# Row maxima on one core: the last two rows in three pieces, and GpSimd on 128-wide parts of ten late rows

## The chip, the cores and the metric

One core of a Trainium2 chip. The time is device microseconds of one execution (us), lower is better. Most executions of a kernel agree within a few tenths of a per cent. So each time is a median of several executions.

## The reference

```python
batch, seq, dim = 32, 512, 1024
x = np.random.randn(batch, seq, dim).astype(np.float32)
return np.max(x, axis=-1).astype(np.float32)
```

That is 16,384 rows of 1024 values, 67.1 MB read and 64 KB written. The kernel lays 128 rows in each of the 128 partitions. In this text "a row" is one row in every partition, 1024 values by 128 partitions, 512 KB.

## The kernel before

SyncE issues 22 loads into a ring of 46 rows, a buffer that is filled over and over. The loads get smaller towards the end. VectorE reduces each load with one instruction. Near the end GpSimd takes five whole rows off VectorE: TensorE transposes the row, ScalarE copies it out of PSUM, the memory that TensorE writes, GpSimd takes the maximum across the partitions, and TensorE brings the result back ("back"), where VectorE reduces eight values per row ("merge").

```python
BLOCKS = [
    [15, 15, 15, 13, 13, 11, 9, 9, 6, 6],
    [3, 3, 2, 1, 1, 1, 1, 1, 1, 1],
]
RING = 46
BY_GPSIMD = {8: 1, 9: 3, 12: 1}        # load: its last rows that GpSimd takes, whole
MERGE = {9: 8, 15: 9, 18: 12}          # after load 9 merge load 8's rows, ...
...
    ring = once.tile([P, RING, D], F32)
    res = once.tile([P, I], F32)
...
            nc.sync.dma_start(out=xc, in_=xb[:, b:b + n, :])
            ...
            reduce = in_turn("DVE", nc.vector.reduce_max(
                out=cols[:, :n - m], in_=xc[:, :n - m, :], axis=X))
...
    half = ring[:, at, :H]
    nc.sync.dma_start(out=half, in_=xb[:, b, :H])
    nc.sync.dma_start(out=tail[:, PAD:], in_=xb[:, b, H:])
    in_turn("DVE", nc.vector.reduce_max(out=tail[:, PAD - 1:PAD], in_=half, axis=X))
    in_turn("DVE", nc.vector.reduce_max(out=res[:, I - 1:], in_=tail[:, PAD - 1:], axis=X))
```

The last row comes in two halves. The maximum of the first half is written just in front of the second, so that one reduction of 513 values finishes the row.

## Time and profile before

| | before |
|---|---|
| time, median (lowest to highest) | 164.42 us (164.33 to 164.50, 3 runs); with later runs of the same kind 164.37 us (6 runs) |
| span of the profiled run | 162.6 us |
| VectorE busy | 135.0 us, 83% |
| load queue busy | 96.6% of the span |
| VectorE idle, waiting for loads | 24.3 us |
| GpSimd busy | 16.3 us |

Two resources are nearly full, the transfers and, from 57 us on, VectorE. The load queue's share says that no other order of the same loads can end much earlier. VectorE's share is an average over a start where it waits and an end where it doesn't. The lines themselves stand in the prediction below.

### The profile page before, as it was taken

To read this page: it belongs to the slowest core of one execution; us is meant where nothing else is said; L and a number is where in the kernel's file an instruction comes from. 1 tells how busy PE (TensorE), PEld (TensorE's weight loads), DVE (VectorE), ACT (ScalarE), POOL (GpSimd) and SP (SyncE) were. 2 spreads that over 40 slices of the span, in tenths; PEclk is the share of its full clock that TensorE was granted. 3 is DMA by queue.
4 is the path that set the end of the run, shared out by engine and by line. 5 is a ranking of instruction groups with operands and counts; after the bars stand their busy time and mean duration, and the time that the engine had idled before them with its cause. 6 is when DMAs were issued, how large, how long until landed. Compare 5 with 4: busy or idle time off the path is not lost.

```text
span 162.6 us, 293 instructions
## 1 busy us (share of the span) xinstructions
PE 13.0 (8%) x80; PEld 11.7 (7%) x80; DVE 135.0 (83%) x33; ACT 6.3 (4%) x6; POOL 16.3 (10%) x9
## 2 busy tenths in 40 slices
PE   0000000000000000000000000000000040943520
PEld 0000000000000000000000000000000030933420
DVE  3000079995999779999996999999999999999994
ACT  3000000000000000000000000000000011240200
POOL 0000000000000000000000000000000007099910
PEclk9999999999999999999999999999999999985555
DMA  7999699988999799999998989999999999999990
GB/s 242 484 484 438 287 484 484 484 378 348 484 484 484 333 498 432 445 419 419 419 419 387 499 388 427 417 426 408 417 435 435 471 399 426 423 418 409 406 368 16
DMA packets 3456, 67.18 MB, mean 413 GB/s; under 512 B 640, under 2 KB 640, under 8 KB 1792
## 3 DMA queue, kind: packets, MB, share of 16 engines
q1 hardware_dynamic: 3168, 67.11, 96.6%
q10 hardware_dynamic: 288, 0.07, 0.2%
HBM read 67.11 MB, written 0.07 MB: 413 GB/s over the span
## 4 chain that ended last, share of the span: by engine, by line
DVE 54%; DMA 44%; SPq 0%; issue 0%
DVE res L139 53%; DMA ring<-in_x_dram 44%; DVE res L156 0%; DVE tail L155 0%; SPq L133 0%; DVE res L143 0%
## 5 line engine op out<-in xcount | busy, mean ns | idle before, releaser
L139 DVE TENSOR_REDUCE res<-ring 128x1 f32<-128x1024 f32 (+6 forms) x20 | 132.1, 6653 | 24.3 <-DMA ring<-in_x_dram 24.3
L106 POOL PARTITION_ALL_REDUCE top<-sb x5 | 16.1, 3255 | 138.8 <-ACT sb L104 138.8
L98 PE MATMUL ps<-ident,ring 128*128 128x128 f32 x40 | 8.1, 382 | 134.2 <-DMA ring<-in_x_dram 131.8
L98 PEld LDWEIGHTS ps<-ident,ring 128*128 128x128 f32 x40 | 7.1, 204 | 134.3 <-issue 134.2
L104 ACT COPY sb<-ps 128x1024 f32<-128x1024 f32 x5 | 5.1, 1013 | 144.9 <-PE ps L98 143.0
L115 PE MATMUL fetched<-ident,top 1*128 1x1 f32 x40 | 5.0, 243 | 9.1 <-POOL top L106 9.1
L115 PEld LDWEIGHTS fetched<-ident,top 1*128 1x128 f32 x40 | 4.6, 214 | 10.3 <-POOL top L106 9.8
L104 ACT ACT_TABLE_LOAD x1 | 1.3, 1283 | 0.7 <-PEq L176 0.7
L76 DVE MEMSET ident<- 128x128 f32 x1 | 0.2, 165 | 0.8 <-PEq L176 0.8
L156 DVE TENSOR_REDUCE res<-tail 128x1 f32<-128x513 f32 x1 | 0.7, 686 | 0.0
L155 DVE TENSOR_REDUCE tail<-ring 128x1 f32<-128x512 f32 x1 | 0.7, 675 | 0.0
L83 DVE TENSOR_SCALAR rowno<-rowno 32x1 f32<-32x1 f32 x3 | 0.4, 147 | 0.1
L143 DVE TENSOR_REDUCE res<-fetched 128x1 f32<-128x8 f32 (+1 forms) x3 | 0.5, 161 | 0.0
L78 DVE TENSOR_TENSOR_SCAN colno<-ident 128x128 f32<-128x128 f32 x1 | 0.4, 425 | 0.0
L85 DVE TENSOR_SCALAR ident<-colno,rowno 128x128 f32<-128x128 f32 x1 | 0.3, 287 | 0.0
L80 DVE STREAM_TRANSPOSE rowno<-colno 128x32 f32<-128x32 f32 x1 | 0.2, 211 | 0.0
L176 POOL MEMSET const-float32-0.0<- 128x1 f32 x1 | 0.1, 99 | 0.2 <-issue 0.2
L176 POOL MEMSET const-uint8-127<- 128x1 uint8 x1 | 0.1, 103 | 0.0
L176 POOL MEMSET const-bfloat16-1.0<- 128x1 bf16 x1 | 0.1, 102 | 0.0
L176 POOL MEMSET const-float32-1.0<- 128x1 f32 x1 | 0.1, 99 | 0.0
L77 DVE MEMSET rowno<- 128x32 f32 x1 | 0.1, 85 | 0.0
## 6 DMA issues: line engine op xcount, KB each, us to landing
ring<-in_x_dram SPq DMA_DIRECT2D x3, 7680.0 KB, 38.4
ring<-in_x_dram SPq DMA_DIRECT2D x2, 6656.0 KB, 34.6
ring<-in_x_dram SPq DMA_DIRECT2D x2, 4608.0 KB, 37.8
ring<-in_x_dram SPq DMA_DIRECT2D x2, 3072.0 KB, 31.9
ring<-in_x_dram SPq DMA_DIRECT2D x1, 5632.0 KB, 28.6
ring<-in_x_dram SPq DMA_DIRECT2D x7, 512.0 KB, 22.3
ring<-in_x_dram SPq DMA_DIRECT2D x2, 1536.0 KB, 34.9
ring<-in_x_dram SPq DMA_DIRECT2D x1, 1024.0 KB, 33.4
```

Of the source, the lines that this page charges most:

```text
L78: in_turn("DVE", nc.vector.tensor_tensor_scan(out=colno, data0=ident, data1=ident, initial=-1.0, op0=ALU.add, op1=ALU.mult))
L83: in_turn("DVE", nc.vector.tensor_scalar(out=part, in0=part, scalar1=float(q * 32), scalar2=None, op0=ALU.add))
L85: in_turn("DVE", nc.vector.tensor_scalar(out=ident, in0=colno, scalar1=rowno[:, 0:1], scalar2=None, op0=ALU.is_equal))
L98: in_turn("PE", nc.tensor.transpose(out=ps[:, c * P:(c + 1) * P], in_=rows[:, k, c * P:(c + 1) * P], identity=ident,))
L104: nc.scalar.copy(out=sb, in_=ps)
L106: nc.gpsimd.partition_all_reduce(top, sb, P, bass_isa.ReduceOp.max)
L115: in_turn("PE", nc.tensor.transpose(out=backs[j][:, k, c:c + 1], in_=tops[j, k][0:1, c * P:(c + 1) * P], identity=ident[0:1, 0:1],))
L139: reduce = in_turn("DVE", nc.vector.reduce_max(out=cols[:, :n - m], in_=xc[:, :n - m, :], axis=X))
L143: in_turn("DVE", nc.vector.reduce_max(out=tiles[i][1], in_=backs[i], axis=X))
L155: in_turn("DVE", nc.vector.reduce_max(out=tail[:, PAD - 1:PAD], in_=half, axis=X))
L156: in_turn("DVE", nc.vector.reduce_max(out=res[:, I - 1:], in_=tail[:, PAD - 1:], axis=X))
L176: nc = _bacc.Bacc("TRN2", target_bir_lowering=False, num_devices=1)
```

## The change

It has four parts. VectorE gets its rows in 21 loads instead of 22, of other sizes. GpSimd takes the first three 128-wide parts (384 of 1024 values) of ten late rows, 3.75 rows' worth, in place of five whole rows, and VectorE the other 640 values. The last two rows come in three pieces of 689, 671 and 688 values, and the middle piece holds the end of one row and the start of the next, so that one reduction with two results serves both. The first store waits for the reduction of the middle piece. The sizes of two buffer pools and the program order of some instructions change with this.

```diff
 BLOCKS = [
-    [15, 15, 15, 13, 13, 11, 9, 9, 6, 6],
-    [3, 3, 2, 1, 1, 1, 1, 1, 1, 1],
+    [15, 15, 15, 13, 11, 9, 8, 5, 8, 7, 6],
+    [4, 3, 2, 2, 1, 1, 1],
 ]
-BY_GPSIMD = {8: 1, 9: 3, 12: 1}
-MERGE = {9: 8, 15: 9, 18: 12}
+SHARED = {10: (5, 3), 12: (3, 3), 14: (2, 3)}    # load: (rows, 128-wide parts)
+MERGE = {13: (10,), 16: (12,), 19: (14,)}
...
+    W = 336
+    K = W - 1
+    AT = I + 16
+    MID = AT + K + W + 17
+    res = once.tile([P, MID + D - W], F32)
...
+        if n > m:
+            maximum(res[:, col:col + n - m], rows(j)[:, :n - m, :])
+        if m and parts < C:
+            maximum(share(j)[:, parts, :], rows(j)[:, n - m:, parts * P:])
+        merge(j)
...
-    half = ring[:, at, :H]
-    nc.sync.dma_start(out=half, in_=xb[:, b, :H])
-    nc.sync.dma_start(out=tail[:, PAD:], in_=xb[:, b, H:])
-    in_turn("DVE", nc.vector.reduce_max(out=tail[:, PAD - 1:PAD], in_=half, axis=X))
-    in_turn("DVE", nc.vector.reduce_max(out=res[:, I - 1:], in_=tail[:, PAD - 1:], axis=X))
+    piece = ring[:, at, :D - K]
+    nc.sync.dma_start(out=piece, in_=xb[:, S - 2, :D - K])
+    pair = xb[:, S - 2:, :].rearrange("p i d -> p (i d)")
+    nc.sync.dma_start(out=res[:, AT:AT + K + W], in_=pair[:, D - K:D + W])
+    nc.sync.dma_start(out=res[:, MID:], in_=pair[:, D + W:])
+    maximum(res[:, AT - 1:AT], piece)
+    latest_row = maximum(
+        bass.AP(tensor=res.tensor, offset=res.offset + I - 2,
+                ap=[list(res.ap[0]), [MID - 1 - (I - 2), 2]]),
+        res[:, AT - 1:AT + K + W].rearrange("p (r k) -> p r k", r=2))
+    merge(len(loads) + 1)
+    maximum(res[:, I - 1:I], res[:, MID - 1:])
```

More of the change, by code (lines that the diff above doesn't have):

```diff
@@ L13 @@
 BLOCKS = [
-    [15, 15, 15, 13, 13, 11, 9, 9, 6, 6],
-    [3, 3, 2, 1, 1, 1, 1, 1, 1, 1],
+    [15, 15, 15, 13, 11, 9, 8, 5, 8, 7, 6],
+    [4, 3, 2, 2, 1, 1, 1],
 ]
 RING = 46
-TENSOR = {
-    8: [("turn", 8, 0), ("back", 8, 0)],
-    9: [("turn", 9, 0), ("turn", 9, 1), ("turn", 9, 2), ("back", 9, 0)],
-    12: [("turn", 12, 0), ("back", 9, 1), ("back", 9, 2), ("back", 12, 0)],
-}
-BY_GPSIMD = {8: 1, 9: 3, 12: 1}
-MERGE = {9: 8, 15: 9, 18: 12}
+SHARED = {10: (5, 3), 12: (3, 3), 14: (2, 3)}
+TENSOR = [
+    ("turn", 10, 0), ("turn", 10, 1), ("turn", 10, 2), ("back", 10, 0),
+    ("back", 10, 1), ("turn", 12, 0), ("turn", 12, 1), ("back", 10, 2),
+    ("turn", 14, 0), ("back", 12, 0), ("back", 12, 1), ("back", 14, 0),
+]
+MERGE = {13: (10,), 16: (12,), 19: (14,)}
 NOSYNC = mybir.DependencyInfo(mybir.DependencyClass.NoSync, mybir.DependencyReason.DATA)
@@ L53 @@
     allr = ctx.enter_context(tc.tile_pool(name="allr", bufs=2))
-    psum = ctx.enter_context(tc.tile_pool(name="psum", bufs=3, space=bass.MemoryType.PSUM))
-    psmall = ctx.enter_context(tc.tile_pool(name="psmall", bufs=2, space=bass.MemoryType.PSUM))
+    psum = ctx.enter_context(tc.tile_pool(name="psum", bufs=2, space=bass.MemoryType.PSUM))
+    psmall = ctx.enter_context(tc.tile_pool(name="psmall", bufs=4, space=bass.MemoryType.PSUM))
     ring = once.tile([P, RING, D], F32)
-    res = once.tile([P, I], F32)
-    PAD = 16
-    tail = once.tile([P, PAD + H], F32)
+    W = 336
[3 more added lines that the diff above has]
+    res = once.tile([P, MID + D - W], F32)
     latest = {}
@@ L86 @@
         out=ident, in0=colno, scalar1=rowno[:, 0:1], scalar2=None, op0=ALU.is_equal))
-    tiles = {}
-    tops = {}
-    backs = {}
-    def turn(j, k):
-        rows, cols = tiles[j]
-        ps = psum.tile([P, D], F32)
-        for c in range(C):
-            in_turn("PE", nc.tensor.transpose(
-                out=ps[:, c * P:(c + 1) * P],
-                in_=rows[:, k, c * P:(c + 1) * P],
-                identity=ident,
-            ))
-        sb = turned.tile([P, D], F32)
-        nc.scalar.copy(out=sb, in_=ps)
-        top = allr.tile([P, D], F32)
-        nc.gpsimd.partition_all_reduce(top, sb, P, bass_isa.ReduceOp.max)
-        tops[j, k] = top
-    def back(j, k):
-        if j not in backs:
-            fetched = psmall.tile([P, BY_GPSIMD[j], C], F32)
-            backs[j] = fetched
-        for c in range(C):
-            in_turn("PE", nc.tensor.transpose(
-                out=backs[j][:, k, c:c + 1],
-                in_=tops[j, k][0:1, c * P:(c + 1) * P],
-                identity=ident[0:1, 0:1],
-            ))
-    at = first = j = 0
+    loads = []
+    first = at = 0
     views = []
-    for loads in BLOCKS:
-        S = sum(loads) + (loads is BLOCKS[-1])
+    for sizes in BLOCKS:
+        S = sum(sizes) + 2 * (sizes is BLOCKS[-1])
         xb = xf[first * P:(first + S) * P, :].rearrange("(p i) d -> p i d", p=P)
@@ L128 @@
         b = 0
-        for n in loads:
+        for n in sizes:
             if at + n > RING:
                 at = 0
-            xc = ring[:, at:at + n, :]
-            nc.sync.dma_start(out=xc, in_=xb[:, b:b + n, :])
-            cols = res[:, first + b:first + b + n]
-            m = BY_GPSIMD.get(j, 0)
-            tiles[j] = xc[:, n - m:, :], cols[:, n - m:]
-            for what, i, k in TENSOR.get(j, []):
-                (turn if what == "turn" else back)(i, k)
-            reduce = in_turn("DVE", nc.vector.reduce_max(
-                out=cols[:, :n - m], in_=xc[:, :n - m, :], axis=X))
-            if j in MERGE:
-                i = MERGE[j]
-                in_turn("DVE", nc.vector.reduce_max(out=tiles[i][1], in_=backs[i], axis=X))
+            loads.append((at, n, xb[:, b:b + n, :], first + b))
@@ L144, with chunks, rows, turn @@
             at += n
             b += n
-            j += 1
         first += S
     assert first == I
+    def chunks(j):
+        m, parts = SHARED[j]
+        per = max(1, C // parts)
+        return [(r, min(per, m - r)) for r in range(0, m, per)]
+    def rows(j):
+        start, n, _, _ = loads[j]
+        return ring[:, start:start + n, :]
+    tops = {}
+    backs = {}
+    def turn(j, c):
+        m, parts = SHARED[j]
+        r, q = chunks(j)[c]
+        W = q * parts * P
+        ps = psum.tile([P, D], F32)
+        for i in range(q):
+            for c0 in range(parts):
+                k = i * parts + c0
+                in_turn("PE", nc.tensor.transpose(
+                    out=ps[:, k * P:(k + 1) * P],
+                    in_=rows(j)[:, loads[j][1] - m + r + i, c0 * P:(c0 + 1) * P],
+                    identity=ident,
+                ))
+        sb = turned.tile([P, D], F32)
+        in_turn("ACT", nc.scalar.copy(out=sb[:, :W], in_=ps[:, :W]))
+        top = allr.tile([P, D], F32)
+        in_turn("POOL", nc.gpsimd.partition_all_reduce(
+            top[:, :W], sb[:, :W], P, bass_isa.ReduceOp.max))
+        tops[j, c] = top
@@ new lines, in share, with back @@
+    def share(j):
+        m, parts = SHARED[j]
+        if j not in backs:
+            fetched = psmall.tile([P, parts + (parts < C), m], F32)
+            backs[j] = fetched
+        return backs[j]
+    def back(j, c):
+        m, parts = SHARED[j]
+        r, q = chunks(j)[c]
+        for i in range(q):
+            for c0 in range(parts):
+                k = i * parts + c0
+                in_turn("PE", nc.tensor.transpose(
+                    out=share(j)[:, c0, r + i:r + i + 1],
+                    in_=tops[j, c][0:1, k * P:(k + 1) * P],
+                    identity=ident[0:1, 0:1],
+                ))
@@ new lines, in maximum, with merge @@
+    def maximum(out, in_):
+        return in_turn("DVE", nc.vector.reduce_max(out=out, in_=in_, axis=X))
+    def merge(j):
+        for i in MERGE.get(j, ()):
+            _, k, _, c0 = loads[i]
+            q, _ = SHARED[i]
+            maximum(res[:, c0 + k - q:c0 + k], share(i).rearrange("p k m -> p m k"))
+    issued = done = 0
+    todo = list(TENSOR)
+    for j in range(len(loads)):
+        while issued < len(loads) and issued < j + 3:
+            start, n, src, _ = loads[issued]
+            held = any(s < start + n and start < s + k for s, k, _, _ in loads[j:issued])
+            if held:
+                break
+            nc.sync.dma_start(out=rows(issued), in_=src)
+            issued += 1
+        while todo and todo[0][1] < (j if todo[0][0] == "back" else issued):
+            what, i, c = todo.pop(0)
+            (turn if what == "turn" else back)(i, c)
+        _, n, _, col = loads[j]
+        m, parts = SHARED.get(j, (0, 0))
+        if n > m:
[3 more added lines that the diff above has]
+        merge(j)
@@ L150 @@
+    for what, i, c in todo:
+        assert what == "back"
+        back(i, c)
     if at + 1 > RING:
         at = 0
-    half = ring[:, at, :H]
-    nc.sync.dma_start(out=half, in_=xb[:, b, :H])
-    nc.sync.dma_start(out=tail[:, PAD:], in_=xb[:, b, H:])
-    in_turn("DVE", nc.vector.reduce_max(out=tail[:, PAD - 1:PAD], in_=half, axis=X))
-    in_turn("DVE", nc.vector.reduce_max(out=res[:, I - 1:], in_=tail[:, PAD - 1:], axis=X))
+    piece = ring[:, at, :D - K]
+    nc.sync.dma_start(out=piece, in_=xb[:, S - 2, :D - K])
@@ new lines @@
+    pair = xb[:, S - 2:, :].rearrange("p i d -> p (i d)")
+    nc.sync.dma_start(out=res[:, AT:AT + K + W], in_=pair[:, D - K:D + W])
+    nc.sync.dma_start(out=res[:, MID:], in_=pair[:, D + W:])
+    maximum(res[:, AT - 1:AT], piece)
+    merge(len(loads))
+    latest_row = maximum(
[3 more added lines that the diff above has]
+    merge(len(loads) + 1)
@@ L159 @@
+    maximum(res[:, I - 1:I], res[:, MID - 1:])
     store = nc.scalar.dma_start(out=views[0][0], in_=views[0][1])
-    tc.add_manual_dep(store.ins, reduce.ins.name, SYNC, reason="behind the loads")
+    tc.add_manual_dep(store.ins, latest_row.ins.name, SYNC, reason="behind the loads")
     nc.scalar.dma_start(out=views[1][0], in_=views[1][1])
```

## The prediction

> **What bounds the kernel now.** I read the page first, then the chain that ended last in order of time, the instructions in order of time (whole run for VectorE, then the last 40 us), the groups by shape, the list of transfers, and the waits of the transfer queue. The page's queue table and its line of rates say that the load queue is occupied for nearly the whole span:
>
> ```profile
> q1 hardware_dynamic: 3168, 67.11, 96.6%
> ```
>
> The chain says who is waited for, and when that changes:
>
> ```profile
> 1.15 38.43 DMA ring<-in_x_dram
> ...
> 55.78 33.41 DMA ring<-in_x_dram
> 89.20 0.03 issue
> 89.22 53.79 DVE res L139 x6
> ```
>
> Until 89.2 us VectorE waits for loads. From there to the end VectorE stands in the chain without a break, so it looks like the bound. It is only just that. VectorE in order of time, and the last two transfers:
>
> ```profile
> 21.46 16.15 DVE L139 TENSOR_REDUCE res<-ring 128x15 f32<-128x15360 f32 x1 [18.95 <-DMA ring<-in_x_dram]
> 39.60 16.15 DVE L139 TENSOR_REDUCE res<-ring 128x15 f32<-128x15360 f32 x1 [1.99 <-DMA ring<-in_x_dram]
> 57.75 30.08 DVE L139 TENSOR_REDUCE res<-ring 128x15 f32<-128x15360 f32 x2 [1.99 <-DMA ring<-in_x_dram]
> 89.22 53.79 DVE L139 TENSOR_REDUCE res<-ring 128x13 f32<-128x13312 f32 x6 [1.40 <-DMA ring<-in_x_dram]
> ...
> 158.97 0.68 DVE L155 TENSOR_REDUCE tail<-ring 128x1 f32<-128x512 f32 x1
> 159.67 0.69 DVE L156 TENSOR_REDUCE res<-tail 128x1 f32<-128x513 f32 x1
> ```
>
> ```profile
> 148.85 0.33 SPq L153 DMA_DIRECT2D ring<-in_x_dram  x1
> ...
> 150.13 0.33 SPq L154 DMA_DIRECT2D tail<-in_x_dram  x1
> ```
>
> The starts at 21.46, 39.60 and 57.75 are moments at which a load landed. A 15-row load (a row is 1024 values in each of 128 partitions, 512 KB) takes 18.14 us. The two issues of the last fence are each released by the landing of an earlier load (the 2-row load, then a 1-row load), so a 1-row load takes 1.28 us. From the two: a transfer costs 1.204 us a row plus 0.076 us a load, and the first load started to count at 21.44 - 18.14 = 3.30 us. Check: 3.30 + 128 x 1.204 + 22 x 0.076 = 159.08 us for the last landing. The list of transfers gives the last half row 9.0 us from its issue at 150.13, that is 159.1. So the stream of loads runs from start to end with no gap that VectorE causes, and its end cannot move by more than the count of loads.
>
> VectorE's own cost, from the groups by shape and from starts in order of time:
>
> ```profile
> L139 DVE TENSOR_REDUCE res<-ring 128x15 f32<-128x15360 f32 x3 | 48.5, 16153 | 22.9 <-DMA ring<-in_x_dram 22.9
> ...
> L139 DVE TENSOR_REDUCE res<-ring 128x1 f32<-128x1024 f32 x8 | 9.4, 1212 | 0.0
> ```
>
> (16.153 - 1.212) / 14 = 1.067 us a row. While there is a backlog one reduction starts 0.083 us before the record of the one before ends, so from start to start it is 1.067 x rows + 0.06 us (one row: 1.126 in the trace). VectorE is 11% faster than the loads, but it can begin a load only when it has landed whole. The last data lands at 159.1, its reduction begins at 159.67 and ends at 160.36: VectorE is 0.55 us late, and 0.69 us of work after the last landing can't be avoided in this form. The stores and the end take 2.3 us more.
>
> **What the Trainium skill says.** "DMA: Bandwidth & Descriptors", section "Where 436 GB/s comes from", puts the ceiling of the transfer fabric at 435 GB/s. The trace agrees: 15 rows in 18.14 us are 7.86 MB / 18.14 us = 433 GB/s. The same page, "How a descriptor splits into AXI transactions", says a transfer that does not start on a 256-byte boundary also fetches the bytes below it. The kernel before has no such source, so no run shows it yet; the middle piece of the change starts 2756 bytes into a row, 196 past a boundary. Estimate from that page: six extra beats on about 84, so 7% of 0.88 us, 0.06 us. "VectorE: DVE Perf Modes", section "The perf-mode tier table (the rule you actually need)", says a reduction runs at one element per cycle whatever its type. The trace agrees: 1024 / 1.067 us = 0.96 elements per ns. The same page, "The DRAIN you can't avoid", says a reduction that reads what the previous one wrote needs a semaphore. The trace shows its price: line 156 starts 0.034 us after line 155 ends instead of 0.083 us before, so 0.117 us.
>
> **The change, part by part.** *Loads.* 22 become 21: 3.30 + 154.11 + 21 x 0.076 = 159.01 us, 0.08 us earlier at most. The real trace runs up to 0.08 us behind this formula late on, so I take late landings 0.08 us later than it.
>
> *GpSimd.* Before it took 5 whole rows (1, 3, 1). Now it takes three eighths of ten rows, 3.75 rows. VectorE therefore gets 1.25 rows more: 1.25 x 1.067 = +1.33 us. The number of VectorE instructions on data stays at 25 (20 + 3 + 2 before; 18 + 1 for the split load, 3 merges, 3 pieces after), so the fixed 0.06 us parts cancel.
>
> *Load sizes.* The load after the first 13 rows shrinks from 13 to 11. It lands at 3.30 + 69 x 1.204 + 5 x 0.076 = 86.8 us, before VectorE is free at 73.82 + 13.93 = 87.75. The 1.40 us wait at 89.2 disappears: this is what pays for the 1.33 us. I then step through every load, start = later of landing and the previous start + 1.067 x rows + 0.06. Starts: 11 rows 87.75, 9 rows 99.5, 8 rows 109.2, 5 rows 117.8, 8 rows 123.2 (landed just then), 7 rows 131.8, the 6-row load 139.4 and its shared part 140.5, 4 rows 143.95 (landing), shared 3 rows 148.3, 2 rows 150.4, shared 2 rows 152.6, single rows 154.0, 155.2 (landing) and 156.47 (landing). The backlog peaks at 4.3 us behind the 5-row load and is gone at the following 8-row load. The same stepping for the kernel before ends at 160.26, where 160.36 was measured.
>
> *The tail.* After 156.47: one row 1.13, first piece (689 wide) 0.78, then the middle one reads what the first wrote, +0.117, so it starts at 158.49. Its 672 elements take 0.76, the last merge 0.08, and the last piece (689 wide) starts at 159.33 and ends 0.80 + 0.06 later, about 160.2. It landed at 159.03, so it is 0.3 us late instead of 0.55; but it is 0.86 us long instead of 0.69. End of the last reduction: 160.36 before, 160.19 after, a gain of 0.17 us. The stores behind it keep their form. 164.42 - 0.17 = 164.25 us.
>
> *Beside other work.* GpSimd's chain for the last shared load: it lands at 152.6, six transposes 1.55, the copy 0.80 + 0.09, the reduction 2.42 if it goes by width (0.75 x 3.23), six transposes back 0.85: ready at 158.4. The merge needs it at 159.25. It is hidden with 0.8 us to spare. The shared load before it is ready near 155.2 for a merge at 156.3.
>
> **The rivals.** First, GpSimd's reduction does not go by width. All five in the trace are 1024 wide and take 3.23 to 3.30 us, so its fixed part is unknown. If a call cost 3.2 us at any width, six in a row from 141.5 would end near 160.4, the merge would be at 161.3 and the end 2 us later, 166.3 us. A fixed part up to about 2 us still hides. Five calls of nearly the same time speak neither way; I give 7% to a visible loss.
>
> Second, the odd pieces move slowly. The middle one has an odd start and crosses from one row into the next. As the middle piece waits for VectorE until 158.49 and lands by the formula at 158.2, the first 0.25 us of any delay is hidden, and the page's 0.06 us with it. If the odd pieces took 30% more, 0.26 us each, the last would land at 159.8 and the end would be about 160.7: 164.8 us. I give 10% to a loss of this kind.
>
> Third, loads into the result tile might wait for VectorE, which writes that tile. The built program's waits speak against it: the two loads wait for queue semaphores alone. It would have cost some 2 us.
>
> Fourth, the tail may gain more: if VectorE caught up everywhere, the end would be 159.03 + 0.02 + 0.86 = 159.9 us, 163.95 us in all. The read-after-write and the 1.13 us of the last whole row stand against it.
>
> **Range and chances.** The stepping missed by 0.1 us on the kernel before, and its three times spread over 0.17 us. So the middle is 164.25, the lower end the fourth rival's 163.95, the upper end half of the second rival's loss, 164.6. Two per cent is 3.3 us: no way that I see gains this, and only a mix of the first rival with something unseen loses it.
>
> **What would show it.** Right: VectorE's waits for loads fall from 24.3 to about 23.1 us; no wait near 88 us; the last reduction starts at about 159.3 and ends at about 160.2; the 128x689 reductions take about 0.86 us; GpSimd's 768-wide calls about 2.4 us. Wrong: VectorE idle before a merge (first rival), a last landing later than 159.2 us (second), transfers into the result tile issued after 157 us (third), a wait for a load after 157 us.

## The result, and the profile after

The changed kernel is correct. It took 164.36 us (164.27 to 164.47, 6 runs), beside 164.37 us for the kernel before (164.22 to 164.50, 6 runs). The ratio is 1.000, with a 95% interval from 0.9987 to 1.0013. No difference shows, and the interval reaches 0.2 us to either side.

| | before | after |
|---|---|---|
| span of the profiled run | 162.6 us | 162.6 us |
| VectorE busy | 135.0 us | 136.4 us |
| VectorE idle, waiting for loads | 24.3 us | 22.9 us |
| GpSimd busy | 16.3 us | 13.0 us |
| load queue busy | 96.6% | 96.6% |

The traces show more than the times. First the queue table of the page (packets, MB, share) and the chain that ended last, in order of time (start, length, what):

```profile
q1 hardware_dynamic: 3024, 67.11, 96.6%
```

```profile
1.15 38.38 DMA ring<-in_x_dram
...
55.70 1.97 another core or an unknown queue
57.67 0.02 issue
57.70 82.85 DVE res L167 x9
140.54 3.40 DVE fetched L167
```

The transfers are as full as before. The chain's second long transfer, 33.4 us and ending at 89.2 us, is gone, and VectorE stands in the chain from 57.7 us on (the line with the unknown queue is the landing of the third load, which the next view names). Its share of the chain went from 54 to 72%, at the same total: a chain's shares say where the chain runs, not what a cut would be worth. VectorE in order of time (start, length, line, operation, then in brackets the idle time before and what ended it), and the issues of the two last pieces:

```profile
21.43 16.15 DVE L167 TENSOR_REDUCE res<-ring 128x15 f32<-128x15360 f32 x1 [18.92 <-DMA ring<-in_x_dram]
39.55 16.15 DVE L167 TENSOR_REDUCE res<-ring 128x15 f32<-128x15360 f32 x1 [1.97 <-DMA ring<-in_x_dram]
57.70 82.85 DVE L167 TENSOR_REDUCE res<-ring 128x15 f32<-128x15360 f32 x9 [1.99 <-DMA ring<-in_x_dram]
...
156.43 2.00 DVE L167 TENSOR_REDUCE res<-ring 128x1 f32<-128x1024 f32 x2
158.47 0.85 DVE L167 TENSOR_REDUCE res<-res 128x2 f32<-128x672 f32 x1
159.24 0.15 DVE L167 TENSOR_REDUCE res<-fetched 128x2 f32<-128x8 f32 x1
159.35 0.87 DVE L167 TENSOR_REDUCE res<-res 128x1 f32<-128x689 f32 x1
```

```profile
143.90 0.33 SPq L205 DMA_DIRECT2D res<-in_x_dram  x1
...
147.60 0.33 SPq L206 DMA_DIRECT2D res<-in_x_dram  x1
```

The wait of 1.40 us before the fifth load has disappeared, and the last reduction starts at 159.35 and ends at 160.23 us. Both pieces are issued more than 10 us before they are needed, so no wait on VectorE holds them. The groups by shape (busy time, mean ns of one):

```profile
L167 DVE TENSOR_REDUCE res<-ring 128x15 f32<-128x15360 f32 x3 | 48.5, 16153 | 22.9 <-DMA ring<-in_x_dram 22.9
...
L142 POOL PARTITION_ALL_REDUCE top<-sb x6 | 12.8, 2181 | 144.5 <-ACT sb L140 144.5
...
L167 DVE TENSOR_REDUCE res<-res 128x1 f32<-128x689 f32 x1 | 0.9, 872 | 0.0
L167 DVE TENSOR_REDUCE res<-ring 128x1 f32<-128x689 f32 x1 | 0.9, 860 | 0.0
L167 DVE TENSOR_REDUCE res<-res 128x2 f32<-128x672 f32 x1 | 0.9, 855 | 0.0
```

**A measure that holds still.** In the fourteen profiles the first reduction starts anywhere from 21.24 to 21.66 us, because the first load lands earlier in one run and later in another, whatever the kernel. Everything behind it moves along. Measured from there, the two profiles of the changed kernel agree to 0.01 us: they have 138.80 and 138.79 us from the start of the first reduction to the end of the last. In the same way the trace's completion events give the time from the first load's landing to the last load's. In the eight profiles that keep the change's three pieces and the ring's place and whose result is right, that time is 137.65 to 137.68 us. I use these two and the stretch behind the last store's landing below. Every kernel but the changed one has a single profile, the kernel before too. For the kernel before they read:

| profile | first reduction's start to last one's end | first load's landing to last one's | last store's landing to end of span |
|---|---|---|---|
| before | 138.90 us | 137.66 us | 0.83 us |
| after | 138.80 us | 137.67 us | 0.90 us |

So VectorE is 0.10 us earlier at the end, the transfers are where they were though one load fewer has its fixed cost, and 0.06 us of the gain is lost behind the last store. (The last store itself takes 1.42 us from issue to landing before and 1.41 us after; that the first store waits for another reduction was not undone alone.) What is left is 0.04 us, a fortieth of a per cent. The experiments take these apart.

### The profile page after: what moved, and what is told of

Read it like the earlier page. It is cut to its first block, busy times and chain, and to the rows that moved or that the text cites. A ratio compares the mean times of both kernels' runs of the same rounds, so it can differ in the third digit from the quotient of the medians.

```text
span 162.6 us, 264 instructions
## 1 busy us (share of the span) xinstructions
PE 10.5 (6%) x60; PEld 9.2 (6%) x60; DVE 136.4 (84%) x33; ACT 5.3 (3%) x7; POOL 13.0 (8%) x10
## 3 DMA queue, kind: packets, MB, share of 16 engines
q1 hardware_dynamic: 3024, 67.11, 96.6%
## 4 chain that ended last, share of the span: by engine, by line
DVE 72%; DMA 24%; another core or an unknown queue 1%; issue 1%; SPq 0%
DVE res L167 68%; DMA ring<-in_x_dram 24%; DVE fetched L167 4%; SPq L184 0%
## 5 line engine op out<-in xcount | busy, mean ns | idle before, releaser
L167 DVE TENSOR_REDUCE res<-ring 128x1 f32<-128x1024 f32 (+10 forms) x17 | 126.2, 7467 | 22.9 <-DMA ring<-in_x_dram 22.9
L142 POOL PARTITION_ALL_REDUCE top<-sb x6 | 12.8, 2181 | 144.5 <-ACT sb L140 144.5
L134 PE MATMUL ps<-ident,ring 128*128 128x128 f32 x30 | 6.9, 415 | 141.9 <-DMA ring<-in_x_dram 141.7
L134 PEld LDWEIGHTS ps<-ident,ring 128*128 128x128 f32 x30 | 5.9, 222 | 142.0 <-issue 142.0
L140 ACT COPY sb<-ps 128x768 f32<-128x768 f32 (+1 forms) x6 | 4.1, 693 | 149.1 <-PE ps L134 147.7
L167 DVE TENSOR_REDUCE fetched<-ring 128x5 f32<-128x3200 f32 (+2 forms) x3 | 7.1, 2376 | 0.0
L160 PE MATMUL fetched<-ident,top 1*128 1x1 f32 x30 | 3.7, 235 | 6.2 <-POOL top L142 6.2
L160 PEld LDWEIGHTS fetched<-ident,top 1*128 1x128 f32 x30 | 3.3, 197 | 7.3 <-POOL top L142 6.9
L167 DVE TENSOR_REDUCE res<-res 128x2 f32<-128x672 f32 (+1 forms) x2 | 1.7, 864 | 0.0
L167 DVE TENSOR_REDUCE res<-fetched 128x5 f32<-128x20 f32 (+2 forms) x3 | 0.5, 161 | 0.0
```

The source lines that it names most:

```text
L134: in_turn("PE", nc.tensor.transpose(out=ps[:, k * P:(k + 1) * P], in_=rows(j)[:, loads[j][1] - m + r + i, c0 * P:(c0 + 1) * P], identity=i ...
L140: in_turn("ACT", nc.scalar.copy(out=sb[:, :W], in_=ps[:, :W]))
L142: in_turn("POOL", nc.gpsimd.partition_all_reduce(top[:, :W], sb[:, :W], P, bass_isa.ReduceOp.max))
L160: in_turn("PE", nc.tensor.transpose(out=share(j)[:, c0, r + i:r + i + 1], in_=tops[j, c][0:1, k * P:(k + 1) * P], identity=ident[0:1, 0:1],))
L167: return in_turn("DVE", nc.vector.reduce_max(out=out, in_=in_, axis=X))
```

## The experiments

The differences below rest on intervals that leave 1 out, and on the traces.

| run | median us | before, same rounds | ratio [95%] | first to last reduction | first to last landing |
|---|---|---|---|---|---|
| again | 164.33 | 164.30 | 1.0004 [0.9991, 1.0018] | 138.79 us | 137.65 us |
| keep13 | 165.46 | 164.30 | 1.0070 [1.0055, 1.0086] | 140.00 us | 137.68 us |
| whole_rows | 165.14 | 164.30 | 1.0050 [1.0038, 1.0063] | 139.59 us | 137.66 us |
| no_share | 167.83 | 164.30 | 1.0216 [1.0202, 1.0230] | 142.36 us | 137.66 us |
| late_pool | 166.05 | 164.30 | 1.0107 [1.0094, 1.0121] | 140.58 us | 137.65 us |
| old_tail | 164.40 | 164.30 | 1.0008 [0.9995, 1.0021] | 138.88 us | 137.59 us |
| floor | 164.10 | 164.30 | 0.9986 [0.9974, 0.9999] | 138.69 us | 137.72 us |
| lane | 164.22 | 164.30 | 0.9994 [0.9982, 1.0007] | 138.80 us | 137.66 us |
| align | 164.30 | 164.30 | 1.0003 [0.9990, 1.0015] | 138.80 us | 137.60 us |
| pad | 163.88 | 164.30 | 0.9976 [0.9962, 0.9989] | 138.47 us | 137.12 us |
| best | 163.96 | 164.30 | 0.9979 [0.9965, 0.9992] | 138.43 us | 137.01 us |
| fast_op | 164.43, one run | 164.30 | | 138.78 us | 137.65 us |

My theory was that both kernels end on the same stream of loads, and that all the change moves is how late VectorE is behind it. The rivals were that the transfers alone set the end, that VectorE's sum of work does, and that the odd pieces cost transfer time.

**The change once more.** No edit.

> The changed kernel, unaltered, timed once more against the kernel before. My theory (both kernels end on the same stream of loads, and the change only moves VectorE's lag behind it): the trace moves the end of the last reduction from 160.36 to 160.23 us, so the ratio should be 0.9990 to 1.0000. Rival (the gain in the trace is chance): ratio 1.000 or above, and the last reduction in this trace not within 0.05 us of 160.23.

The ratio was 1.0004, so the times neither show a gain nor exclude 0.1 us of one. The last reduction ended at 160.36 us, which looks like the kernel before and is outside the 0.05 us that I had set; but the first reduction started at 21.56 in this run, and from there it took 138.79 us, as in the first profile.

**The load sizes: the wait at 88 us brought back.**

```diff
-    [15, 15, 15, 13, 11, 9, 8, 5, 8, 7, 6],
+    [15, 15, 15, 13, 13, 9, 8, 3, 8, 7, 6],
```

> The change with 13 rows instead of 11 in the fifth load and 3 instead of 5 in the eighth, so that the wait before the fifth load that the kernel before has comes back. Theory: VectorE waits about 1.4 us near 88 us again, keeps 1.3 to 1.5 us more lag to the end, last reduction near 161.4 us, total +1.25 us (about 165.6). Rival (the wait at 88 us is idle time that costs nothing, as the loads are the bound): no change beyond 0.2 us.

VectorE in order of time:

```profile
57.57 30.08 DVE L167 TENSOR_REDUCE res<-ring 128x15 f32<-128x15360 f32 x2 [1.99 <-DMA ring<-in_x_dram]
89.06 52.77 DVE L167 TENSOR_REDUCE res<-ring 128x13 f32<-128x13312 f32 x7 [1.41 <-DMA ring<-in_x_dram]
...
160.44 0.87 DVE L167 TENSOR_REDUCE res<-res 128x1 f32<-128x689 f32 x1
```

The wait of 1.41 us is back, and the last reduction ends 1.20 us later relative to the first (140.00 against 138.80). The time went up by 1.1 us. Idle time 70 us before the end is not free here: behind it VectorE is never idle long enough to catch up. This is the part that pays for giving GpSimd 1.25 rows less.

**GpSimd's parts: the same loads with whole rows.** GpSimd takes three whole rows of the 6-row load and one of the 3-row load.

```diff
-SHARED = {10: (5, 3), 12: (3, 3), 14: (2, 3)}
+SHARED = {10: (3, 8), 12: (1, 8)}
...
-MERGE = {13: (10,), 16: (12,), 19: (14,)}
+MERGE = {14: (10,), 17: (12,)}
```

> Loads and tail of the change, but GpSimd takes four whole rows (three of the 6-row load, one of the 3-row load) instead of 128-wide parts of ten rows that come to 3.75 rows. Theory (relief before the last moment at which VectorE waits for a landing is lost as idle time): VectorE idles about 1.3 us before the 4-row load at 143.9 us and the last reduction ends near 161.1 us, some 0.85 us later, although VectorE has a quarter row less to do. Rival (only the sum of VectorE's work counts): it ends 0.2 us earlier, near 160.0 us.

VectorE in order of time, its last wait for a load:

```profile
143.78 11.00 DVE L166 TENSOR_REDUCE res<-ring 128x4 f32<-128x4096 f32 x4 [1.23 <-DMA ring<-in_x_dram]
```

VectorE has a quarter row less to do than in the change and ends 0.79 us later. The relief comes where VectorE is ahead of the loads anyway, so 1.23 us of it turns into idle time, and the rows after it have none. The 128-wide parts spread the same work over ten rows up to the last 2-row load. The rival, that the sum of work counts, falls.

**GpSimd's part taken away.**

```diff
-SHARED = {10: (5, 3), 12: (3, 3), 14: (2, 3)}
+SHARED = {}
```

> The change with nothing given to GpSimd: VectorE reduces all 128 rows. Theory by stepping: VectorE is 3.9 us behind at the end, last reduction near 163.9 us, the whole about 168.0 us (+3.66). The loads still end at 159.1 us. Rival (the transfers alone set the end): under 0.5 us longer.

VectorE in order of time:

```profile
57.64 104.31 DVE L163 TENSOR_REDUCE res<-ring 128x15 f32<-128x15360 f32 x17 [1.99 <-DMA ring<-in_x_dram]
161.98 1.76 DVE L163 TENSOR_REDUCE res<-res 128x2 f32<-128x672 f32 x2
```

The loads end as always (137.66 us from first to last landing), VectorE runs without a break from 57.6 us to 163.74 us, and the time is 3.5 us longer. So the loads alone do not set the end. VectorE's 3.75 rows are 4.0 us at 1.067 us a row, less about 0.3 us for the three merges and the split that go with them; 3.56 us of it show (142.36 against 138.80).

**GpSimd's chain made late.** One unused 768-wide reduction ahead of GpSimd's last one (two buffers were cut from 1024 to 768 columns to make room).

```diff
...
+        if (j, c) == (14, 0):
+            in_turn("POOL", nc.gpsimd.partition_all_reduce(
+                spare[:, :W], sb[:, :W], P, bass_isa.ReduceOp.max))
+        top = allr.tile([P, 768], F32)
```

> The change with one more 768-wide GpSimd reduction, its result unused, ahead of the last one. Theory (GpSimd's chain is hidden with about 0.65 us to spare): the last transposes back end 2.4 us later, near 161.0 us, the last merge waits for them, and the last reduction ends about 1.75 us later, near 162.0 us. If the chain had much more to spare than the trace shows (a merge that does not really wait): no change. If GpSimd were already the bound: 2.4 us later.

In order of time:

```profile
155.14 2.50 POOL L143 PARTITION_ALL_REDUCE spare<-sb  x1 [1.10 <-ACT sb L141]
...
157.55 2.58 POOL L146 PARTITION_ALL_REDUCE top<-sb  x1
...
161.01 0.17 DVE L171 TENSOR_REDUCE res<-fetched 128x2 f32<-128x8 f32 x1 [1.75 <-PE fetched L164]
161.09 0.87 DVE L171 TENSOR_REDUCE res<-res 128x1 f32<-128x689 f32 x1
```

2.4 us more on GpSimd made the last merge wait 1.75 us, so 0.65 us of GpSimd's chain was spare. It is hidden in the change, but not by much.

**The tail as before**, with the change's loads and parts.

```diff
-    [4, 3, 2, 2, 1, 1, 1],
+    [4, 3, 2, 2, 1, 1, 1, 1],
...
+    nc.sync.dma_start(out=half, in_=xb[:, S - 1, :H])
+    nc.sync.dma_start(out=res[:, AT:AT + H], in_=xb[:, S - 1, H:])
+    latest_row = maximum(res[:, AT - 1:AT], half)
+    maximum(res[:, I - 1:I], res[:, AT - 1:AT + H])
```

> Loads and GpSimd's parts of the change, but the last two rows as before: one whole row and two halves (21 loads still). Theory by stepping: the last reduction ends 0.15 us later than in the change, near 160.4 us, because the first half waits for the whole row's reduction and the second for the first's result. Rival (the tail's gain is the shorter last piece: 513 against 689 wide): 0.18 us earlier, near 160.05 us.

VectorE in order of time:

```profile
159.01 0.68 DVE L167 TENSOR_REDUCE res<-ring 128x1 f32<-128x512 f32 x1
159.72 0.69 DVE L167 TENSOR_REDUCE res<-res 128x1 f32<-128x513 f32 x1
```

With two halves the last reduction ends 0.08 us later than with three pieces (138.88 against 138.80). The sign is the theory's and the size half of its 0.15. The rival of a shorter last piece falls. A side result matters more: with 21 loads and even halves the stream is 137.59 us long, 0.07 us less than with 22 loads. The change has 21 loads as well and its stream is 137.67 (137.65 to 137.68 in the runs with the same three pieces).

**Where the three pieces are cut.** 704, 641 and 703 values.

```diff
-    W = 336
+    W = 321
-    MID = AT + K + W + 17
+    MID = AT + K + W + 47
```

> The change with its last three pieces cut at other places, 704, 641 and 703 values, so that the middle one starts on a 256-byte boundary of the input and the last 4 bytes past one. Theory (the odd starts cost 0.08 us of transfer time, which is what the 22nd load had cost): from the landing of the first load to that of the last 137.60 to 137.63 us, against 137.67 in the change and in the kernel before, and 137.59 with the old tail. Rival (the odd lengths cost it, or nothing does): 137.67.

The stream was 137.60 us. So the places of the cuts cost the change 0.07 us of transfer time, as much as the load that it saved. The completion events put it where the edit is: from the landing of the last whole row to that of the last piece it took 2.59 us, against 2.67 (2.65 to 2.70 in the eight profiles), while the last whole row landed 135.01 us after the first load in both. The end of the last reduction didn't move (138.80), because VectorE, not the last landing, is what the last reductions wait for.

**The floor under VectorE.** VectorE reads 64 columns of each row only; the result is wrong (relative error 0.31), and the last three pieces are untouched.

```diff
-            maximum(res[:, col:col + n - m], rows(j)[:, :n - m, :])
+            maximum(res[:, col:col + n - m], rows(j)[:, :n - m, :64])
...
-            maximum(share(j)[:, parts, :], rows(j)[:, n - m:, parts * P:])
+            maximum(share(j)[:, parts, :], rows(j)[:, n - m:, parts * P:parts * P + 64])
```

> The change with VectorE reading only 64 columns of each row, except in the three last pieces (wrong result on purpose). What is left is the stream of loads and the last three reductions. Theory: last landing still 159.1 us, the last reduction ends near 160.0 us, 0.2 us earlier than in the change; so all of VectorE's work of 130 us costs 0.2 us. Rival (VectorE is the bound, as the chain's 72% has it): more than 1 us earlier. A third possibility, that reading by VectorE slows the loads: the last landing comes before 158.8 us.

VectorE in order of time:

```profile
156.34 0.22 DVE L167 TENSOR_REDUCE res<-ring 128x1 f32<-128x64 f32 x1 [0.96 <-DMA ring<-in_x_dram]
157.26 0.87 DVE L167 TENSOR_REDUCE res<-ring 128x1 f32<-128x689 f32 x1 [0.71 <-DMA ring<-in_x_dram]
...
159.12 0.87 DVE L167 TENSOR_REDUCE res<-res 128x1 f32<-128x689 f32 x1
```

With next to nothing to do before the tail, VectorE ends 0.11 us earlier (138.69 against 138.80), half of what I had expected. Almost all of VectorE's work in the change therefore lies beside the transfers, though the chain gives VectorE 72%. The stream was 137.72 us, so VectorE's reading doesn't slow the loads.

**The stretch behind the last store.** One 64-byte transfer more, ahead of the loads, and nothing else.

```diff
+    spare = once.tile([P, 16], F32)
+    nc.scalar.dma_start(out=spare[0:1, :], in_=xf[0:1, :16])
```

> The change with one 64-byte transfer more, ahead of the loads, so that there are 24 transfers again as in the kernel before, and the last store gets the last of the eight transfer semaphores. Theory (part of the change's gain is given back at the very end: SyncE goes through its semaphores in their order, and with 23 transfers it still has one to look at, long satisfied, after the last store has landed): from the landing of the last store to the end of the span 0.84 us as before, instead of 0.90; the rest unchanged; total shorter by 0.06 us. Rival (the 0.06 us is chance): 0.90 us again.

From the last store's landing to the end of the span it took 0.83 us again. The trace shows why. The transfers use eight semaphores in turn, and at the end SyncE looks at each of them in a fixed order. With 24 transfers the last store has the last semaphore. With the change's 23 it has the last but one, and SyncE begins to look at the last, long satisfied, 0.06 us after it has seen the store (at 161.69 and 161.75 us). The time, 164.22 us, fits 0.06 us but does not separate it from the change's; the trace does.

**Another instruction for the reduction.** The first single-row load by an elementwise maximum that also accumulates.

```diff
...
+        if j == 15:
+            in_turn("DVE", nc.vector.tensor_scalar(
+                out=scratch, in0=rows(j)[:, 0, :], scalar1=-3.0e38, scalar2=-3.0e38,
+                op0=ALU.max, op1=ALU.max, accum_out=res[:, col:col + 1]))
```

> The change with the first single-row load reduced by an elementwise maximum against a constant that also accumulates the maximum, instead of a reduction. If that instruction reads two elements per cycle, it takes about 0.7 us instead of 1.21 us, and a faster tail is to be had; if one, about 1.2 us or more.

The groups by shape:

```profile
L193 DVE TENSOR_SCALAR_CACHE_REDUCE scratch<-ring 128x1024 f32<-128x1024 f32 x1 | 1.2, 1208 | 0.0
L193 DVE DVE_READ_ACCUMULATOR scratch<-ring 128x1 f32 x1 | 0.1, 82 | 0.0
```

It takes 1.21 us as a reduction does, and a read of the accumulator besides. There is no faster tail this way.

**Where the ring starts.** In both kernels the ring and the result tile start 128 bytes past a 256-byte boundary of their partition (the address in the built program is 16,512). A 128-byte tile ahead of them moves both to a boundary.

```diff
+    pad = once.tile([P, 32], F32)
     ring = once.tile([P, RING, D], F32)
```

> The change with 128 bytes of padding ahead of the ring, so that the ring and the result tile start on a 256-byte boundary; in both kernels they start 128 bytes past one. Theory (a write that starts off the boundary costs beats as a read does; part of the 0.076 us that each load costs beside its bytes is that): [...]the stream from first to last landing shortens by about 0.65 us, to 137.0 us, and the total by 0.6 us. Rival (only the source counts): 137.67 us and no change.

VectorE in order of time:

```profile
57.47 82.76 DVE L168 TENSOR_REDUCE res<-ring 128x15 f32<-128x15360 f32 x9 [1.99 <-DMA ring<-in_x_dram]
...
158.84 0.87 DVE L168 TENSOR_REDUCE res<-res 128x1 f32<-128x689 f32 x1
```

Of the kernels with a right result, this one and the last below, which contains it, are the only ones whose interval lies under 1: 163.88 us, ratio 0.9976, interval 0.9962 to 0.9989. The packet records say where it comes from. A packet of 4096 bytes (one row of one partition) takes 159.0 ns in the mean, against 162.8 in the change. Packets up to 32 KB are 3 to 4 ns shorter, longer ones are the same. The stream is 0.56 us shorter (my 0.65 had counted the long packets too); the packets account for some 0.5 of it. VectorE passes on 0.33 of it (138.47 against 138.80): the time from the last landing to the end of the last reduction grew from 1.15 to 1.38 us, so now VectorE is what lags. Beside the kernel before, the trace has 0.37 us (138.90 less 138.47, less the 0.06 behind the last store) and the times 0.42, which agrees within the interval.

**Everything together**: the padding, the better cuts with their places on boundaries, and the small transfer.

```diff
+    pad = once.tile([P, 32], F32)
-    W = 336
+    W = 321
-    AT = I + 16
-    MID = AT + K + W + 17
+    AT = I + 64
+    MID = AT + K + W + 63
+    spare = once.tile([P, 16], F32)
+    nc.scalar.dma_start(out=spare[0:1, :], in_=xf[0:1, :16])
```

> The extra small transfer, the better cuts and the padding together, the pieces' places in the result tile on 256-byte boundaries too. If all three theories hold: about 0.75 us shorter than the change, 163.6 us. If the padding does nothing: 0.1 to 0.15 us shorter, the last reduction ending 0.05 us earlier relative to the first landing.

It was 163.96 us, 0.2% faster than the kernel before, and not distinguishable from the padding alone. I had expected 163.6. The trace has 138.43 us between the reductions, 0.04 less than with the padding alone, and 0.83 us behind the last store. The better cuts gave nothing more here: the last three landings took 2.60 us, against 2.59 with the padding alone. The stream is 0.11 us shorter, but it was so by the sixth landing (76.07 against 76.18 us), long before the three pieces, in which alone their loads differ, so this isn't the cuts' doing. Its profiled run had the latest first reduction (21.66 us), which hides the rest in the time. The kernel to keep is the padded one, whose gain the times themselves show.

## Why the prediction was right or wrong

The predicted 164.25 us lies 0.11 us from the measured 164.36, well inside the range, and "within 2%" was right. That is little to be proud of: the range held "no change" as well, and the starting value of 164.42 us came down to 164.37 with three more runs, so that part of the closeness is luck. The direction, 0.17 us faster, is not in the times. In the traces the mechanism can be tested. Step by step:

**The stream of loads.** The last landing came at 159.08 us, predicted as 159.03, and the floor, no_share and late_pool show that VectorE and GpSimd don't move it (137.65 to 137.72 us from first to last landing). The 0.08 us "at most" for the saved load was not had: the stream is as long as before, because the cuts of the three pieces cost about as much (old_tail and align are 0.05 to 0.09 us shorter than the eight profiles). I had counted 0.06 us for the middle piece's start and called it hidden behind VectorE. Hidden it was: with better cuts the end of the last reduction stayed.

**VectorE, load by load.** Right. Predicted starts of 87.75, 99.5, 109.2, 117.8, 123.2, 131.8, 139.4, 143.95, 148.3 and 156.47 us were measured as 87.69, 99.48, 109.14, 117.74, 123.21, 131.81, 139.34, 143.91, 148.25 and 156.43. Idle time on loads fell to 22.9 us, predicted 23.1. That the wait at 89 us is worth most of its length, and pays for nearly all of the 1.25 rows, is shown by keep13: 1.41 us of wait cost 1.20 us at the end.

**The tail.** The end of the last reduction was predicted 138.73 us after the first one's start and came at 138.80. The term that was mis-sized is "the last merge 0.08": it is 0.12 us from the merge's start to the last reduction's. The last reduction reads what the middle one wrote and starts 0.034 us after that one's end, as line 156 did before, and the merge between them shortens nothing. In late_pool, where the middle one had ended long before the merge, the last reduction does start 0.08 us after the merge's start (161.01 and 161.09 us), so the wait for the middle one's result is the cause. The other 0.03 us are three terms of 0.01 (1.137 for the whole row, 0.77 for the middle, 0.872 for the last). So the gain was 0.10 us, not 0.17.

**The end.** "The stores behind it keep their form" failed. With 23 transfers the last store is no longer on the last semaphore, and 0.06 us are given back (lane). Of 0.10 us 0.04 stay, which no set of times here could show.

**The rivals.** GpSimd's reduction goes mostly by width: 2.50 us for 768 and 1.50 us for 384 values, against 3.23 us for 1024, so some 0.3 to 0.5 us of a call is fixed. (The sum for this rival was off: six calls of 3.2 us from 141.5 end at 160.7, not 160.4.) Its chain was hidden with 0.65 us to spare, predicted 0.8. Loads into the result tile waited for earlier loads (4.6 and 3.4 us), not for VectorE. The fourth rival, that VectorE might catch up everywhere, was bounded by the floor at 0.11 us; I had given it 0.3.

**What stays open.** Why the three cuts cost 0.07 us. The packet records narrow it down. Moving the ring to a boundary shortens the first piece's packets by 3.2 ns, and those of the three pieces of align by 2.6 to 3.3 ns (align against best, where the places in the result tile move too); all of these start on a boundary of the input or 4 bytes past one. It shortens the change's two other pieces by more: the middle one, which starts 196 bytes past a boundary, from 114.3 to 107.0 ns, and the last, which starts 64 bytes past one, from 116.9 to 109.0. The 4.5 ns more are 0.07 us over the 16 packets of an engine, as much as the cuts cost. So a start off the boundary of the input cost something where the destination was 192 and 128 bytes past one, as in the change, and nothing that shows where it was 64 and 0 bytes past one, as in the padded kernel. Why, and why 64 bytes of the input cost as much as 196, is not shown. Only one offset of the ring, 128 bytes, was tried against none.

## What to carry to other kernels

When transfers and an engine are both full to the end, a tuned tail is flat: the load sizes and GpSimd's parts move the time by about a microsecond when one is undone alone (keep13 1.2 us, whole_rows 0.8 us in the traces), the tail by 0.08 us, and all of them together by 0.10. Judge such a change from an event that does not scatter (here the first reduction's start), and count what follows the last result, too. Before more tuning of sizes, look at where the tiles start: 128 bytes of padding gave more than the whole change, though the load queue had looked full at 96.6%: a queue's share says that it is busy, not that its packets are as short as they can be.

## What the Trainium skill lacked or had wrong

- "DMA: Bandwidth & Descriptors", section "How a descriptor splits into AXI transactions", tells of reads that start off a 256-byte boundary. It says nothing of where the write starts. Here a ring 128 bytes past a boundary made each 4096-byte packet 3.8 ns longer (162.8 against 159.0 ns) and the stream of loads 0.56 us, while an odd start in the input showed no cost of its own in the padded kernel (107.0 ns for 2684 bytes, where the line of the others gives 107 to 108). The estimate of 0.06 us for the middle piece that I took from it had the size of what the cuts cost (0.07 us), but not its parts: in the change the starts of the middle and the last piece cost 0.03 to 0.04 us each, and in the padded kernel nothing that shows.
- The section that the prediction cites for the ceiling, "Where 436 GB/s comes from" of the same page, also says that loads from HBM are bound by the HBM side at about 358 GB/s. For one core alone that was not so here: 15 rows came at 433 GB/s.
- "VectorE: DVE Perf Modes", section "The perf-mode tier table (the rule you actually need)", gives the elementwise operation with a scalar two fp32 elements per cycle and doesn't tell the accumulating form apart. The skill has that elsewhere: "SBUF — State Buffer", section "Who interferes with whom", leaves the form that writes out its accumulator out of the two-port modes. The run agrees: 1208 ns for 1024 values, as a reduction. Neither has the 82 ns to read the accumulator.
- No page gives the cost of GpSimd's maximum across partitions by width: 1.50 us for 384, 2.50 us for 768, 3.23 us for 1024 values. "GPSIMD Engine Reference", section "3.2 Cross-partition — where GPSIMD wins", has one time for another instruction, a reduction along the partition axis at 2048 values, of 248 us; the one used here is far from it.
- No page has the 0.06 us that SyncE takes at the end of this program for a transfer semaphore behind that of the last store.
